# Channel-major projections: high and low part of the activations as one 512-column moving operand, small vectors loaded as rows, a ring of four weight buffers

## The chip, the cores and the metric

The kernel runs on one NeuronCore of a Trainium2 chip. The metric is the device time of one execution in microseconds (us), the median of several runs.

The engines that matter are the tensor engine (PE; its loads of stationary operands are listed as PEld), the vector engine (DVE), the scalar engine (ACT), GpSimd (POOL) and the queue of the sync engine (SP), which issues nearly all transfers. Each takes its instructions in the order in which they stand in the program.

## The reference, cut to what matters

Two blocks follow each other, each with two layers, on 256 rows of width 1024, all in fp32. The first block has three attention branches, the second a mixer with three branches and a gated feed-forward part.

```python
# first block, layer l: x is 256 x 1024
h = rms_norm(x, norm_g[l])
q_a, k_a, v_a, q_h, f_h, i_h, q_m, z = split(h @ w_in[l])        # 512 columns each, z 1536
o_h = hgrn2_chunkwise(q_h, f_h, i_h, lb_all[l])                  # wants q_h and f_h with channels on partitions
kv_m = rms_norm(mem, mem_norm_g[l]) @ w_mem_kv[l]
x = x + (concat([o_a, o_h, o_m]) * silu(z)) @ w_out[l]

# second block, layer l
h = rms_norm_2(x, mix_pre_norm[l])
dn_qkv, dn_z, dn_b, dn_a, ret_q, ret_k, ret_v, ret_g, pool_u, gates = split(h @ w_in[l])
qkv = silu(causal_depthwise_conv(dn_qkv, dn_conv[l]))            # four taps along the rows, per channel
o_dn = gated_delta_rule(q, k, v, beta, g); ...                   # and retention, pooling
x = x + rms_norm_2(mixed @ w_out[l], ...);  x = x + rms_norm_2(swiglu(...), ...)
```

## The kernel before

**Products.** Every fp32 product is made of three matmuls on rounded parts: high weight times high activation, low times high, high times low. The activations stand transposed in SBUF as `aTh` (high) and `aTl` (low), channels on the partitions. `tok` products have the rows of x on the output partitions and move 512 weight columns per matmul. `chan` products have output channels on the partitions: the weight is the stationary operand, 128 channels at a time, and the 256 rows of `aTh` or `aTl` move. `chan` is called ten times: for f_h and then q_h in each layer of the first block, and for k, q and v of the gated delta branch (`dn_k`, `dn_q`, `dn_v`) in each layer of the second.

**One chan call.** It takes four weight units of 256 input by 512 output channels, and its 512 output channels are four blocks of 128. Two blocks share one PSUM bank. The call goes over the four units twice, once for each pair of blocks; a unit comes free in the second pass. After a pass the work on the result (`evac`: `hgrn_f`, `silu`, `conv_silu`) is queued, and reads the bank in PSUM. `conv_silu` makes for each block one ACT instruction with the first tap and three DVE instructions with the others, then a clamp and a silu.

**Weights.** `Stream` brings 412 units of 512 KB in a fixed order. SP loads a unit into one of five raw buffers; ACT copies it, rounded, to `wh`; DVE subtracts to give `wl`; PE uses both. There are six slots for such pairs, with two spare ones for some units. The slot of a unit is free for another when the last matmul on it is done. A raw buffer is free when its `wl` is done.

**What sets the order.** The class `Order` plans as the program is written: each piece of work on ACT and DVE is a generator that yields the tiles it needs, and is stepped when the planned time of PE has come so far. `pump` writes the splits of the weights among them. A scheduler then moves instructions within each engine, matmuls of two PSUM banks among each other as well.

**Small vectors.** Gains, convolution taps and the like are loaded with one element per partition (`(k p) -> p k`), most of them by SP between the weight loads, the first gain by POOL. `lower_bounds` and `mem_norm` load theirs about 40 us into the execution, `mixer2` loads `dn_conv`, `dn_out_norm` and `pool_scale` for its layer.

Of the kernel before, what the change touches and what calls it, by code (L numbers as in the profile page):

```python
# [35 lines left out]
K4, K2, SM, ACC = 11, 22, 24, 3  # L36
# [194 lines left out]
class Stream:  # L231
# [5 lines left out]
    RAW, SLOTS, SPARE, AHEAD = 5, 6, 2, 6  # L237
# [130 lines left out]
class Kernel:  # L368
# [50 lines left out]
    def part(self):  # L419

        return tuple(self.t(self.p_aT, [P, 4, S], tag, F32R) for tag in ("aTh", "aTl"))
# [121 lines left out]
    def norm(self, x, gb, hT, t, ss=None, gc=None):  # L543
# [19 lines left out]
        for b in range(2):  # L563
# [4 lines left out]
            for k in range(4):  # L568
                g = gc[:, 4 * b + k : 4 * b + k + 1]
                h, l = (y[:, k, t * P : (t + 1) * P] for y in hT[b])  # L570
# [61 lines left out]
    def tok(self, hT, keys, evac, own=True, wait=None, first=False):  # L632
# [4 lines left out]
        for t in range(NT):  # L637
# [4 lines left out]
            for key in keys:  # L642
                ps = self.acc()
                for u in range(nu):
                    if t == 0:
                        w[key, u] = self.stream.take((key, u))
                    for k in range(2):
                        kk = 2 * u + k
                        self.mm3(ps, tuple(x[:, kk % 4, t * P : (t + 1) * P] for x in hT[kk // 4]),
                                 tuple(x[:, k, :] for x in w[key, u]), kk == 0, kk == 2 * nu - 1)  # L650
# [5 lines left out]
    def chan(self, hT, key, evac):  # L656

        self.join_hT(0, 1)
        nu, ku, nj = KD // 2, 2, 4
        w = []  # L660
        for p in range(nj // 2):
            pt = self.acc((P, 2, S))
            for u in range(nu):
                if p == 0:
                    w.append(self.stream.take((key, u)))
                wh, wl = w[u]
                for k in range(ku):
                    kk = u * ku + k
                    xh, xl = (x[:, kk % 4, :] for x in hT[kk // 4])
                    for j in range(2):  # L670
                        c = slice((2 * p + j) * P, (2 * p + j + 1) * P)
                        o = pt[:, j, :]
                        first = kk == 0 and j == 0
                        last = kk == nu * ku - 1 and j == 1
                        self.pe.matmul(o, wh[:, k, c], xh, start=first, stop=False, skip_group_check=True)
                        self.pe.matmul(o, wl[:, k, c], xh, start=False, stop=False, skip_group_check=True)
                        self.pe.matmul(o, wh[:, k, c], xl, start=False, stop=last, skip_group_check=True)
                    self.o.poll()
                if p == nj // 2 - 1:
                    self.stream.free()  # L680
            self.o.spawn(evac(p, pt))
            self.o.poll()

    def out_proj(self, parts, skew, evac):
# [7 lines left out]
        def mm(t, n, i):  # L692
# [6 lines left out]
            for kk in range(2):  # L699
                xs = tuple(o[:, 2 * k + kk, t * P : (t + 1) * P] for o in oT)  # L700
# [56 lines left out]

    def constants(self):

        a, dve = self.a, self.dve  # L760
        neg = self.k2([P, 2 * P], "stage")
# [57 lines left out]
    def lower_bounds(self):  # L819

        l0, l1, d, e = (self.cst([P, 4], n) for n in ("lb0", "lb1", "lbd", "lbe"))
        for l, t in enumerate((l0, l1)):
# [1068 lines left out]
```

## Time and profile before

| | |
|---|---|
| median of 3 runs | 1415.88 us (1415.46 to 1416.79) |
| the profiled execution | 1414.58 us |
| its span, first to last instruction | 1412.7 us |
| PE busy | 1383.5 us (98%), 7604 matmuls |
| DVE busy | 1017.0 us (72%) |
| ACT busy | 829.4 us (59%) |
| granted TensorE clock, mean | 0.999 |

Matmuls overlap: the mean duration of one in a list of groups is longer than the distance from its start to the start of the next. PE's pace is read from the starts in a timeline. A row of the timeline can stand for several equal instructions in a row (x2 and so on); its start is that of the first. PEclk 0.999 is the upper of the clock's two levels, 2.4 GHz, in nearly the whole span.

### The profile page before, as it was taken

The page shows a single profiled execution, that of the slowest core. Times are in us where ns is not written, and L with a number is a line of the kernel's source. Part 1 is how long each engine was busy: PE and PEld are TensorE (multiplying, and loading weights), DVE is VectorE, ACT ScalarE, POOL GpSimd, SP SyncE. Part 2 cuts the span into 40 slices and gives each one's busy share as a digit, 9 for nine tenths or more (in the row PEclk, how much of TensorE's full clock was granted, in tenths as well). Part 3 has the DMA queues.
Part 4 walks back from the last instruction along what each step waited for, and adds up shares of the span by engine and source line. Part 5 has one row for each costly group of instructions (what it writes and reads, how often), then busy time and mean ns, then how long its engine had stood idle before and what let it go on. Part 6 is the DMA issues. An engine that isn't in the chain of part 4 may idle for free.

```text
span 1412.7 us, 20443 instructions
## 1 busy us (share of the span) xinstructions
PE 1383.5 (98%) x7604; PEld 1164.6 (82%) x7604; DVE 1017.0 (72%) x1708; ACT 829.4 (59%) x1420; POOL 31.4 (2%) x66
## 2 busy tenths in 40 slices
PE   7999999999999999999999999999999999999998
PEld 5878888887888898888877888879888887788886
DVE  6698777679887698657777655687968567666564
ACT  6676565566765476556755544565665466555452
POOL 7100000000000000000000000000000000000000
PEclk9999999999999999999999999999999999999999
DMA  8863446555345354235665656645544357365551
GB/s 271 216 152 101 122 138 218 165 158 170 118 146 181 117 181 136 89 90 179 205 198 164 190 185 194 220 138 175 152 118 120 98 184 253 120 202 186 182 187 64
DMA packets 140916, 229.06 MB, mean 162 GB/s; under 512 B 28304, under 2 KB 34064, under 8 KB 140816
## 3 DMA queue, kind: packets, MB, share of 16 engines
q1 hardware_dynamic: 140752, 227.75, 52.2%
q8 instruction: 60, 0.98, 0.3%
q0 software_dynamic: 64, 0.01, 0.1%
q14 instruction: 40, 0.33, 0.1%
HBM read 226.67 MB, written 1.05 MB: 161 GB/s over the span
## 4 chain that ended last, share of the span: by engine, by line
PE 79%; DVE 6%; DMA 5%; ACT 4%; issue 3%; SPq 1%; DVEq 0%; ACTq 0%
PE acc L137 54%; PE mx L137 21%; PE mx L147 4%; DVE wl L109 3%; ACT wh L109 2%; DMA raw<-in_w_in 2%; DMA raw<-in_w_out 1%; DMA raw<-in_ffn_gate 1%; SPq L408 1%; ACT sg L109 1%; ACT junk L109 1%; DMA gqk<-in_moba_q_norm 0%; DVE x L109 0%; DVE hlf L109 0%; DMA stage<-in_c_negs 0%
## 5 line engine op out<-in xcount | busy, mean ns | idle before, releaser
L109 DVE TENSOR_TENSOR wl<-raw,wh 128x1024 fp32r<-128x1024 f32 x396 | 479.8, 1220 | 145.2 <-ACT wh L109 139.1
L109 ACT CAST wh<-raw 128x1024 fp32r<-128x1024 f32 x396 | 412.6, 1049 | 173.3 <-PE acc L137 91.9
L137 PE MATMUL acc<-wh,aTh 128*128 128x512 f32 x1232 | 494.6, 402 | 2.7 <-ACT aTh L109 2.6
L137 PE MATMUL acc<-wl,aTh 128*128 128x512 f32 x1232 | 485.2, 394 | 0.2 <-DVE wl L109 0.2
L137 PE MATMUL acc<-wh,aTl 128*128 128x512 f32 x1232 | 483.8, 393 | 1.0 <-DVE aTl L109 1.0
L137 PEld LDWEIGHTS acc<-wh,aTh 128*128 128x128 f32 x1232 | 232.1, 188 | 50.0 <-ACT aTh L109 4.8
L137 PEld LDWEIGHTS acc<-wh,aTl 128*128 128x128 f32 x1232 | 231.9, 188 | 49.7 <-DVE aTl L109 2.3
L137 PEld LDWEIGHTS acc<-wl,aTh 128*128 128x128 f32 x1232 | 232.3, 189 | 45.1 <-issue 1.0
L137 PE MATMUL mx<-wh,ff 128*128 128x512 f32 x352 | 111.2, 392 | 0.0
L137 PE MATMUL acc<-aTh,wh 128*128 128x256 f32 x320 | 91.0, 284 | 0.0
L137 PE MATMUL acc<-aTl,wh 128*128 128x256 f32 x320 | 90.6, 283 | 0.0
L137 PE MATMUL acc<-aTh,wl 128*128 128x256 f32 x320 | 90.5, 283 | 0.0
L137 PEld LDWEIGHTS mx<-wh,ff 128*128 128x128 f32 x352 | 65.6, 188 | 13.2
L109 ACT ACTIVATE sg<-sg 128x512 f32<-128x512 f32 (+1 forms) x120 | 73.7, 614 | 1.5
L109 ACT ACTIVATE sg<-zc 128x512 f32<-128x512 f32 (+1 forms) x60 | 37.0, 616 | 61.6 <-DVE zc L109 61.3
L137 PE MATMUL mx<-wl,ff 128*128 128x512 f32 x176 | 68.5, 389 | 0.0
L137 PEld LDWEIGHTS acc<-aTh,wh 128*128 128x128 f32 x320 | 61.3, 192 | 0.3
L137 PEld LDWEIGHTS acc<-aTh,wl 128*128 128x128 f32 x320 | 61.3, 192 | 0.2
L137 PEld LDWEIGHTS acc<-aTl,wh 128*128 128x128 f32 x320 | 61.3, 192 | 0.0
L109 DVE TENSOR_SCALAR zc<-acc 128x512 f32<-128x512 f32 (+1 forms) x48 | 31.9, 664 | 36.8 <-PE acc L137 36.8
L109 ACT CAST ff<-mx 128x256 fp32r<-128x256 f32 x44 | 14.4, 375 | 52.8 <-PE mx L147 52.8
L109 ACT CAST aTh<-mx 128x512 fp32r<-128x512 f32 x44 | 24.7, 585 | 31.9 <-PE mx L147 31.6
(313 smaller groups left out, 1656.0 us busy)
## 6 DMA issues: line engine op xcount, KB each, us to landing
raw<-in_w_in SPq DMA_DIRECT2D x200, 512.0 KB, 4.3
raw<-in_ffn_down SPq DMA_DIRECT2D x44, 512.0 KB, 4.8
raw<-in_w_out SPq DMA_DIRECT2D x40, 512.0 KB, 4.5
raw<-in_ffn_gate SPq DMA_DIRECT2D x40, 512.0 KB, 4.6
raw<-in_ffn_up SPq DMA_DIRECT2D x40, 512.0 KB, 4.5
raw<-in_w_mem_kv SPq DMA_DIRECT2D x16, 512.0 KB, 4.5
raw<-in_w_branch_pool SPq DMA_DIRECT2D x8, 512.0 KB, 3.7
raw<-in_w_branch_ret SPq DMA_DIRECT2D x8, 512.0 KB, 4.0
```

The costliest lines, as they stand in the source:

```text
L109: r = f(out, *args, **kw)
L137: self._ns.matmul(out, lhsT, rhs, **kw)
L147: self._ns.transpose(out, x, ident)
L408: self.nc.sync.dma_start(dst, src)
```

## The change

The high and low part of the activations become one tile, `aT`, with both parts next to each other for each group of 128 channels. In `chan` one matmul moves both parts, 512 columns, over the high weight, and a second moves the 256 columns of the high part over the low weight into the first half of the bank. A block now fills one bank by itself, so the call goes over its four units four times, and a unit comes free in the fourth pass. The two halves of a bank are added by the new `halves_sum`: ACT copies the first half to SBUF, DVE adds the second. The evac then reads SBUF; `hgrn_f` drops the copy that it made before.

`columns` loads vectors as rows of 128 into one tile, transposes them on PE and copies them out with DVE. It takes the place of nearly all loads with one element per partition; the first gain moves from the queue of POOL to that of SP. The ring of raw buffers goes from five to four, the pool of small tiles from 22 to 24.

```diff
-K4, K2, SM, ACC = 11, 22, 24, 3
+K4, K2, SM, ACC = 11, 24, 24, 3
...
-    RAW, SLOTS, SPARE, AHEAD = 5, 6, 2, 6
+    RAW, SLOTS, SPARE, AHEAD = 4, 6, 2, 6
...
-        return tuple(self.t(self.p_aT, [P, 4, S], tag, F32R) for tag in ("aTh", "aTl"))
+        x = self.t(self.p_aT, [P, 4, 2, S], "aT", F32R)
+        return x[:, :, 0, :], x[:, :, 1, :], x
...
-        for p in range(nj // 2):
+        for j in range(nj):
+            if j % 2 == 0:
+                self.uid += 1
+                banks, ready, out = [], f"chan{self.uid}", self.k2([P, 2, S], "chan")
             pt = self.acc((P, 2, S))
+            banks.append(pt)
+            c = slice(j * P, (j + 1) * P)
...
-                    xh, xl = (x[:, kk % 4, :] for x in hT[kk // 4])
-                    for j in range(2):
-                        c = slice((2 * p + j) * P, (2 * p + j + 1) * P)
-                        o = pt[:, j, :]
-                        first = kk == 0 and j == 0
-                        last = kk == nu * ku - 1 and j == 1
-                        self.pe.matmul(o, wh[:, k, c], xh, start=first, stop=False, skip_group_check=True)
-                        self.pe.matmul(o, wl[:, k, c], xh, start=False, stop=False, skip_group_check=True)
-                        self.pe.matmul(o, wh[:, k, c], xl, start=False, stop=last, skip_group_check=True)
+                    x = hT[kk // 4][2][:, kk % 4]
+                    self.pe.matmul(pt, wh[:, k, c], x, start=kk == 0, stop=False, skip_group_check=True)
+                    self.pe.matmul(pt[:, 0, :], wl[:, k, c], x[:, 0, :], start=False, stop=kk == nu * ku - 1, skip_group_check=True)
...
-                if p == nj // 2 - 1:
+                if j == nj - 1:
                     self.stream.free()
-            self.o.spawn(evac(p, pt))
+            if j % 2:
+                self.o.done.add(ready)
+            else:
+                self.o.spawn(self.chain(self.halves_sum(banks, ready, out), evac(j // 2, out)))
...
+    def halves_sum(self, banks, ready, out):
+        for j in range(2):
+            if j:
+                yield ready
+            yield banks[j]
+            self.act.copy(out[:, j, :], banks[j][:, 0, :])
+            yield out
+            self.dve.tensor_tensor(out[:, j, :], banks[j][:, 1, :], out[:, j, :], op=ALU.add)
+        yield out
...
+    def columns(self, dst, srcs):
+        r, n = self.k2([P, P], "rows"), 0
+        for src in srcs:
+            self.load(r[n : n + src.shape[0], :], src)
+            n += src.shape[0]
+        yield r
+        tp = self.mx((P, n))
+        self.pe.transpose(tp, r[:n, :], self.ident[:n, :n])
+        yield tp
+        self.dve.tensor_copy(dst[:, :n], tp)
+        yield dst
...
-        f, e, lf = self.k2(sh, "hf"), self.k2(sh, "he"), self.k2(sh, "hlf")
-        act.copy(f, ps)
-        yield f
+        f, e, lf = ps, self.k2(sh, "he"), self.k2(sh, "hlf")
...
-        for j in range(4):
-            self.load(cw[:, j, :], a["dn_conv_2"][l, j].rearrange("(i p) -> p i", p=P))
-        self.load(lay[:, 48:49], a["dn_out_norm_2"][l].unsqueeze(1))
-        self.load(lay[:, 60:64], a["pool_scale_2"][l].rearrange("(n p) -> p n", p=P))
+        o.spawn(self.columns(lay, [a["dn_conv_2"][l, j].rearrange("(i p) -> i p", p=P) for j in range(4)]
+                             + [a["dn_out_norm_2"][l : l + 1], a["pool_scale_2"][l].rearrange("(n p) -> n p", p=P)]), f"lay{l}")
...
-        self.nc.gpsimd.dma_start(gc, a["norm_g" if self.depth1 else "mix_pre_norm_2"][0].rearrange("(k p) -> p k", p=P))
-        o.ready[gc.name] = 4000.0
+        cols = self.columns(gc, [a["norm_g" if self.depth1 else "mix_pre_norm_2"][0].rearrange("(k p) -> k p", p=P)])
+        next(cols)
```

**On PE,** in the first layer of the second block, at the start of the call for `dn_v`. The numbers behind the names tell tiles apart; `acc` is a PSUM bank. Before, the call's first matmuls on its first unit (wh_5292 and wl_5293) read:

```order
L137 MATMUL acc_5459<-aTh_4723,wh_5292 128x256
L137 MATMUL acc_5459<-aTh_4723,wl_5293 128x256
L137 MATMUL acc_5459<-aTl_4724,wh_5292 128x256
L137 MATMUL acc_5459<-aTh_4723,wh_5292 128x256
L137 MATMUL acc_5459<-aTh_4723,wl_5293 128x256
L137 MATMUL acc_5459<-aTl_4724,wh_5292 128x256
```

After, the units of this call are 5168, 5179, 5270 and 5286, its blocks 5307, 5341, 5362 and 5390. Its first block at the third and fourth unit reads:

```order
L137 MATMUL acc_5307<-aT_4625,wh_5270 128x512
L137 MATMUL acc_5307<-aT_4625,wl_5271 128x256
L137 MATMUL acc_5307<-aT_4625,wh_5270 128x512
L137 MATMUL acc_5307<-aT_4625,wl_5271 128x256
L137 MATMUL acc_5341<-aT_4624,wh_5168 128x512
L137 MATMUL acc_5307<-aT_4625,wh_5286 128x512
L137 MATMUL acc_5341<-aT_4624,wl_5169 128x256
L137 MATMUL acc_5341<-aT_4624,wh_5168 128x512
...
L137 MATMUL acc_5307<-aT_4625,wl_5287 128x256
```

Three matmuls have become two, and seven matmuls of the second block (acc_5341) stand among those of the first block on the fourth unit, six of them between its high and its low weight.

**On ACT,** around the splits of the third and fourth unit of the same call, while PE ends the call for `dn_q`. Before (third and fourth unit: 5398, 5422; the two after them belong to the next product):

```order
L109 ACTIVATE conv_5370<-acc_5308,lay_4857 128x256 x2
L109 CAST wh_5398<-raw_5123 128x1024
L109 CAST wh_5422<-raw_5266 128x1024
L109 ACTIVATE sg_5408<-zc_5407 128x512
L109 CAST wh_5437<-raw_5290 128x1024
L109 ACTIVATE sg_5408<-sg_5408 128x512
L109 CAST wh_5452<-raw_5341 128x1024
L109 ACTIVATE sg_5408<-sg_5408 128x512
```

After (third and fourth unit: 5270, 5286):

```order
L109 COPY chan_5236<-acc_5237 128x256
L109 ACTIVATE sg_5274<-zc_5273 128x512
L109 CAST wh_5270<-raw_5164 128x1024
L109 ACTIVATE sg_5274<-sg_5274 128x512
L109 ACTIVATE conv_5281<-chan_5184,lay_4756 128x256
L109 ACTIVATE sg_5274<-sg_5274 128x512
L109 ACTIVATE conv_5281<-chan_5184,lay_4756 128x256
L109 CAST wh_5286<-raw_5189 128x1024
L109 CAST wh_5296<-raw_5198 128x1024
L109 CAST wh_5301<-raw_5218 128x1024
L109 COPY chan_5236<-acc_5262 128x256
```

The two casts stood next to each other; now four instructions of silu and convolution stand between them, and the copy of the fourth block of `dn_q` (acc_5262) stands behind three more casts.

**On DVE,** at the same place. Before:

```order
L109 TENSOR_TENSOR wl_5399<-raw_5123,wh_5398 128x1024
L109 SCALAR_TENSOR_TENSOR conv_5370<-acc_5308,lay_4857,conv_5370 128x254
L109 TENSOR_TENSOR wl_5423<-raw_5266,wh_5422 128x1024
L109 SCALAR_TENSOR_TENSOR conv_5370<-acc_5308,lay_4857,conv_5370 128x253
L109 TENSOR_TENSOR wl_5438<-raw_5290,wh_5437 128x1024
```

After:

```order
L109 TENSOR_TENSOR wl_5271<-raw_5164,wh_5270 128x1024
L109 SCALAR_TENSOR_TENSOR conv_5281<-chan_5184,lay_4756,conv_5281 128x255
L109 TENSOR_TENSOR cvk_5001<-zc_5273,sg_5274 128x512
L109 SCALAR_TENSOR_TENSOR conv_5281<-chan_5184,lay_4756,conv_5281 128x254
L109 SCALAR_TENSOR_TENSOR conv_5281<-chan_5184,lay_4756,conv_5281 128x255
L109 TENSOR_TENSOR wl_5287<-raw_5189,wh_5286 128x1024
L109 TENSOR_TENSOR wl_5297<-raw_5198,wh_5296 128x1024
L109 SCALAR_TENSOR_TENSOR conv_5281<-chan_5184,lay_4756,conv_5281 128x253
L109 SCALAR_TENSOR_TENSOR conv_5281<-chan_5184,lay_4756,conv_5281 128x254
L109 TENSOR_TENSOR wl_5302<-raw_5218,wh_5301 128x1024
L109 SCALAR_TENSOR_TENSOR conv_5281<-chan_5184,lay_4756,conv_5281 128x253
L109 TENSOR_TENSOR chan_5236<-acc_5262,chan_5236 128x256
```

One instruction of the convolution stood between the low parts of the third and fourth unit; now four instructions do. The sum that empties the bank acc_5262 stands behind three low parts and six others.

## Rows read from the trace of the kernel before

**Rows 1.** The page's first lines: span; busy time, share and count by engine.

```profile
span 1412.7 us, 20443 instructions
PE 1383.5 (98%) x7604; PEld 1164.6 (82%) x7604; DVE 1017.0 (72%) x1708; ACT 829.4 (59%) x1420; POOL 31.4 (2%) x66
```

**Rows 2.** Waits of PE: line, awaited engine: us in total, times, longest.

```profile
PE mx L147 <- DVE xn L109: 11.2, 6, 7.2
...
PE acc L137 <- DVE wl L109: 0.2, 1, 0.2
```

**Rows 3.** Timeline of PE, dn_q to dn_v: start, duration, instruction.

```profile
505.77 0.28 PE L137 MATMUL acc<-aTh,wl 128*128 128x256 f32 x1
...
506.49 0.28 PE L137 MATMUL acc<-aTh,wl 128*128 128x256 f32 x1
...
507.93 0.28 PE L137 MATMUL acc<-aTh,wl 128*128 128x256 f32 x1
```

**Rows 4.** Timeline of PE, a tok product of the first layer.

```profile
23.83 0.39 PE L137 MATMUL acc<-wh,aTh 128*128 128x512 f32 x1
...
26.10 0.62 PE L137 MATMUL acc<-wh,aTh 128*128 128x512 f32 x2
```

**Rows 5.** Groups by line and shape: count | busy us, mean ns | idle before.

```profile
L137 PE MATMUL acc<-wh,aTh 128*128 128x512 f32 x1232 | 494.6, 402 | 2.7 <-ACT aTh L109 2.6
...
L137 PE MATMUL acc<-aTh,wh 128*128 128x256 f32 x320 | 91.0, 284 | 0.0
...
L109 DVE TENSOR_TENSOR ff<-mx,ff 128x256 fp32r<-128x256 f32 x44 | 16.8, 420 | 21.1 <-ACT ff L109 21.1
...
L109 ACT CAST ff<-mx 128x256 fp32r<-128x256 f32 x44 | 14.4, 375 | 52.8 <-PE mx L147 52.8
...
L109 ACT COPY hf<-acc 128x512 f32<-128x512 f32 x4 | 2.3, 573 | 4.7 <-PE acc L137 4.7
```

**Rows 6.** Timeline of ACT, second pass of dn_q and first of dn_v.

```profile
499.37 1.05 ACT L109 CAST wh<-raw 128x1024 fp32r<-128x1024 f32 x1 [0.60 <-PE acc L137]
500.81 1.05 ACT L109 CAST wh<-raw 128x1024 fp32r<-128x1024 f32 x1 [0.39 <-PE acc L137]
501.76 0.63 ACT L109 ACTIVATE sg<-zc 128x512 f32<-128x512 f32 x1
...
505.73 0.63 ACT L109 ACTIVATE sg<-zc 128x512 f32<-128x512 f32 x1 [0.39 <-DVE zc L109]
506.26 0.46 ACT L109 ACTIVATE conv<-acc,lay 128x256 f32<-128x256 f32 x1
...
507.50 0.63 ACT L109 ACTIVATE sg<-sg 128x512 f32<-128x512 f32 x1
```

**Rows 7.** Timeline of DVE, the same stretch.

```profile
501.09 1.21 DVE L109 TENSOR_TENSOR wl<-raw,wh 128x1024 fp32r<-128x1024 f32 x1
502.23 0.47 DVE L109 SCALAR_TENSOR_TENSOR conv<-acc,lay,conv 128x254 f32<-128x254 f32 x1
502.62 1.21 DVE L109 TENSOR_TENSOR wl<-raw,wh 128x1024 fp32r<-128x1024 f32 x1
...
505.61 0.68 DVE L109 TENSOR_TENSOR cvk<-zc,sg 128x512 f32<-128x512 f32 x1
506.21 1.21 DVE L109 TENSOR_TENSOR wl<-raw,wh 128x1024 fp32r<-128x1024 f32 x1
```

**Rows 8.** Busy us of each engine by stretch, count; clock, DMA share, GB/s.

```profile
500.00:512.00 12.00, 12.00 (x102) 12.00 (x101) 11.55 (x22) 9.23 (x15) 0.00 (x0) 1.00 0.57 176
```

**Rows 9.** Timeline of all engines, the first 12.5 us.

```profile
1.25 1.09 POOL L1790 DMA_DIRECT2D gain<-in_norm_g  x1 [0.82 <-POOLq L1880]
1.63 0.42 SPq L408 DMA_DIRECT2D ident<-in_c_ident  x1
...
9.56 1.04 ACT L109 CAST wh<-raw 128x1024 fp32r<-128x1024 f32 x1 [3.49 <-DMA raw<-in_w_in]
...
11.94 0.79 PE L137 MATMUL acc<-wl,aTh 128*128 128x512 f32 x1 [0.22 <-DVE wl L109]
```

**Rows 10.** Timeline of PE, the transposes for the norm of mem.

```profile
54.89 0.88 PE L147 MATMUL mx<-ident,xn 128*128 128x128 f32 x6 [1.68 <-DVE xn L109]
```

More of the change, by code (lines that the diff above doesn't have):

```diff
@@ L569, in norm @@
                 g = gc[:, 4 * b + k : 4 * b + k + 1]
-                h, l = (y[:, k, t * P : (t + 1) * P] for y in hT[b])
+                h, l = (y[:, k, t * P : (t + 1) * P] for y in hT[b][:2])
                 self.act.activation(h, tp[b][:, k, :], AF.Copy, scale=g)
@@ L648, in tok @@
                         kk = 2 * u + k
-                        self.mm3(ps, tuple(x[:, kk % 4, t * P : (t + 1) * P] for x in hT[kk // 4]),
+                        self.mm3(ps, tuple(x[:, kk % 4, t * P : (t + 1) * P] for x in hT[kk // 4][:2]),
                                  tuple(x[:, k, :] for x in w[key, u]), kk == 0, kk == 2 * nu - 1)
@@ L699, in mm @@
             for kk in range(2):
-                xs = tuple(o[:, 2 * k + kk, t * P : (t + 1) * P] for o in oT)
+                xs = tuple(o[:, 2 * k + kk, t * P : (t + 1) * P] for o in oT[:2])
                 self.mm3(pss[t][i], xs, tuple(w[:, kk, :] for w in ws[n, i]),
@@ L756, in masks @@
         return t
+    def columns(self, dst, srcs):
[9 more added lines that the diff above has]
+        yield dst
     def constants(self):
         a, dve = self.a, self.dve
+        L = self.depth1
+        cut = lambda x: x.rearrange("(n p) -> n p", p=P)
+        c = self.cst([P, 32], "cols")
+        srcs = []
+        for l in range(L):
+            srcs += [a["mem_q_norm"][l : l + 1], a["mem_k_norm"][l : l + 1], a["hgrn_o_norm"][l : l + 1], cut(a["mem_norm_g"][l])]
+        srcs += [cut(a["hgrn_lb_logits"][l]) for l in range(2)]
+        yield from self.columns(c, srcs)
+        self.mem_qk, self.ogain = [c[:, 11 * l : 11 * l + 2] for l in range(L)], [c[:, 11 * l + 2 : 11 * l + 3] for l in range(L)]
+        self.mem_gain = [c[:, 11 * l + 3 : 11 * l + 11] for l in range(L)]
+        self.lb = [c[:, 11 * L + 4 * l : 11 * L + 4 * l + 4] for l in range(2)]
+        self.o.done.add("cols")
         neg = self.k2([P, 2 * P], "stage")
@@ L871, in mem_norm @@
     def mem_norm(self, mT):
-        self.mem_gain = [self.cst([P, KD], f"memgain{l}") for l in range(self.depth1)]
-        for l, x in enumerate(self.mem_gain):
-            self.load(x, self.a["mem_norm_g"][l].rearrange("(k p) -> p k", p=P))
         for m in range(NT):
@@ L925, in layer1 @@
         ss = [self.sm(16, "qkss") for _ in range(NT)]
+        if not l:
+            o.join("cols")
         for n, x in enumerate("qk"):
@@ L1389, in dn_scalars @@
         for k in range(KD):
-            xh, xl = (x[:, k % 4, :] for x in hT[k // 4])
+            xh, xl = (x[:, k % 4, :] for x in hT[k // 4][:2])
             pe.matmul(ps, wh[:, k, :], xh, start=k == 0, stop=False)
```

17 lines of the change are left out of this document (7 added, 10 removed).

## The prediction

> **What bounds the kernel now.** I read the page's first lines, then what PE waits for, then timelines. PE is busy for 1383.5 of 1412.7 us [rows 1]; DVE at 72% and ACT at 59% are not the bound over the whole span. PE's waits are few: 11.2 us for `xn`, most of it the 7.2 us before the first transposes, and in the whole execution 0.2 us for a `wl` [rows 2]. So time is won only by giving PE less to do, and lost wherever something that was ready in time comes late. The profiled execution took 1414.58 us, its span 1412.7, so 1.9 us lie around the span; the median of the three runs, 1415.88, is 1.3 us above it. I work out differences and put them to the median.
>
> **The products.** Read from mean durations, the gain would be large: three matmuls at 284 ns are 852 ns, and 402 plus 284 are 686 [rows 5]; times 320 that is 53 us. But durations overlap: the pace is the distance between starts. In the `dn_q` to `dn_v` stretch 18 matmuls of 256 columns go from 505.77 to 507.93 us [rows 3]: 2.16/18 = 0.120 us each. In a `tok` product 10 of 512 go from 23.83 to 26.10 [rows 4]: 0.227 us each. Three of 256 are 0.360, one of 512 with one of 256 is 0.347. The 768 columns are the same; what falls away is what each matmul costs beyond its columns, 0.013 us. Rows 5 count 320 triples, so PE saves 320 x 0.013 = **4.2 us**, 0.3%, all of it on the path, since PE does not wait in this stretch (12.00 of 12 us busy [rows 8]).
>
> The Trainium skill, TensorE: Matmul & The Clock Gate, Back-to-back issue gap, gives an isolated warm gap of N/2.4 + 2.5 ns, so 215.8 ns for 512 and 109.2 for 256, and an estimate from that page is a saving of 2.5 ns a triple, 0.8 us in all. The rows show 227 and 120 ns, the trace does not agree, and I keep 4.2 us.
>
> **The slots of the weights.** The price is in the passes. Before, PE spent 12 matmuls, 1.44 us, on a unit in each of two passes; a unit's slot came free in the second pass, and the third unit of the next call, which takes the slot of the first of this one, was wanted five such steps later, 7.2 us. The rows show it: its cast starts at 499.37 just after PE lets go [rows 6], its low part takes 1.21 from 501.09 [rows 7] and ends at 502.30, and PE uses it at 506.49 [rows 3], 4.2 us later. The low part of the fourth unit ends at 503.83 [rows 7] for 507.93 [rows 3], 4.1 us. After, a unit takes 2 x 0.347 = 0.694 us of each of four passes, it is free in the fourth only, and five steps are 3.5 us. Of 4.2 and 4.1 us about 0.5 is left, for the same work on ACT and DVE. This holds at six transitions: f_h to q_h in two layers, k to q and q to v in two.
>
> And the work is not the same. Each call gets four copies of 128x256 from PSUM and four sums of that size, at 375 and 420 ns by the nearest rows, the `ff` copies and subtractions [rows 5]. For ten calls that is 15.0 us of ACT and 16.8 of DVE; only four `hf` copies of 573 ns go, 2.3 us [rows 5]. In the delta calls DVE is busy for 11.55 of 12 us already [rows 8], so 1.7 us more in each call must push something behind.
>
> I walked the changed order at `dn_q` to `dn_v`, first layer, with steps from start to start: cast 0.95 (500.81 to 501.76), silu, tap, silu, tap together 1.77 (505.73 to 507.50) [rows 6]; low part 1.14, convolution step 0.39, `cvk` 0.60 [rows 7]. Zero is the end of the third block of `dn_q`. Its slots come free at 0.69 and 1.39; PE wants the third unit of `dn_v` at 4.16, the fourth at 4.86. ACT first copies, then a silu waits for a clamp that DVE reaches at about 1.0, behind six convolution steps. The first cast runs from 1.6 to 2.6, its low part to 3.8: in time. The four small instructions between the casts bring the second to 4.4 to 5.4, its low part to 6.7. PE has one matmul of the next block to put in between, then waits 0.3 us for the cast; six more reach to about 6.7. Without them it would wait 1.8. Then the bank: the third block of `dn_v` needs the bank of acc_5262, whose sum stands behind two low parts and three convolution steps, 6.7 + 2 x 1.14 + 3 x 0.39 + 0.42 = 10.6, while PE comes there at about 9.2, after two more blocks and some small products of the retention. That is 1.4 us, so 1.7 at this transition.
>
> The same walk gives about 1.1 us at q to v in the second layer (the low parts of two units stand behind twelve convolution steps), 0.7 at q_h in the first layer, and 0.4 more before the transposes for the norm of mem, where DVE, in order, now also waits for the transpose of the vectors ahead of the `xn` that PE waits for [rows 10]. At k to q, and at q_h in the second layer, I find next to nothing. Sum: **+3.9 us**. The bounds are 0, if DVE runs half a microsecond less behind at each place, and 10.1 us, if all of the added 1.7 us of DVE in six calls lands on PE. I take the walk, nearer to the lower end, since it goes by the rows of the same stretch.
>
> **Vectors, ring and start.** The loads as rows add four transposes, some 0.1 us each as one of 256 columns is 0.12 [rows 3]: +0.4. The first gain now stands on SP behind `ident` and ahead of the first two weight transfers, one issue of 0.42 us [rows 9]. PE's first matmul on a low part, at 11.94, follows from the landing of the first weight, which ended ACT's wait at 9.56 [rows 9]; so up to +0.4. Against it, the gather of the first gain with 4-byte elements on POOL's queue (issued from 1.25 [rows 9]) no longer shares the engines; between -0.4 and +0.4 I take -0.1. Later small loads lie under waits of SP that cost nothing. Four buffers for five would make 35 of 412 casts start later when I replay SP's issues with landing times of the trace, but nearly all of these have microseconds of lead left: 0, with +1 as the upper end. Two more small tiles free nothing that PE waits for. Sum: **+0.3 us**.
>
> **The forecast** is -4.2 + 3.9 + 0.3 = 0.0 us: **1415.9 us**, no change. About 0.2%, 2.8 us, is what a measurement of this kernel can tell from none.
>
> **The rivals.**
>
> (a) The waits do not appear. For it: before, `wl` cost PE 0.2 us in all [rows 2], each wait I found is of about the size of the error in DVE's lag, and six hoisted matmuls already cover one. The evac also leaves PSUM earlier, since it reads SBUF. Against it: the slot's time is halved by arithmetic. It gives -4.2 + 0.3, with at most 1 us of waits: 1412 to 1413. Chance 0.32.
>
> (b) DVE becomes PE's bound in the calls, and the kernel is slower. The mechanism is one: a sum of 0.42 us stands in order between the low parts, and once a low part comes after its use, every later instruction of DVE in the call is on PE's path, as there is 0.45 us of idle in 12 [rows 8] against 1.7 us added. It decides when the 0.5 us of lead left per unit is gone at all six transitions. All of it: -4.2 + 10.1 + 0.3 = +6.2, 1422.1; two thirds of it +2.8. So 1418.7 to 1422. Chance 0.20.
>
> (c) The vectors or the four buffers hurt: a transpose of rows holds DVE or PE at the start of a mixer or in the first 60 us until the rows have landed, 3 us or more, since a late landing is also late for the splits queued behind on DVE. 1419. Chance 0.05.
>
> (d) The saving itself is other. If the 0.013 us belonged to something that stays, such as the change of the moving width between 512 and 256, PE would save nothing, and the waits would be left: 1420. Chance 0.03. If the mean durations did count, 53 us: 1363; the row sums of overlapping matmuls speak against it. Or a 512-column matmul next to a 256-column one could run faster than in rows 4: at the pace of 256 columns for both, 0.240 for 0.360, 38 us. Chance 0.01 for these two together. The last is beside a rule of the Trainium skill, TensorE: Matmul & The Clock Gate, Back-to-back issue gap, by which a stream with weight loads takes about 131 ns for N=512. The 227 ns here, in such a stream, do not agree.
>
> (e) The change does what it says: 640 matmuls stand where 960 did, in the order as built, so I give nothing to its not happening.
>
> **How the numbers follow.** The forecast case, 1413 to 1418.7, has 0.39. Faster by over 0.2% is (a) with nearly all its part below 1413.1, and the small part of (d): 0.33. Slower is (b), (c) and the rest of (d): 0.28. The range of 8 in 10 reaches from 1411.5, a little below (a), to 1421, inside (b).
>
> **What the profile of after would show.** Right on the products: rows of 512 and 256 columns, x320 each, starts 0.347 us apart per pair. Right on the slots: PE waits for `wl`, `wh` or the sum on `chan`, 2 to 6 us in all, at `dn_q` to `dn_v` (near 504 and 981 us) and q_h; leads of some 0.5 us where there were 4. (a) shows no such rows, and the span shorter by 4. (b) shows the waits at all six, above 7 us, with DVE at 98% there. (c) shows waits for `rows` or a copy behind them. The prediction is wrong if the starts are not 0.347 apart, or if PE's waits for the split weights and banks in these calls come to under 1 us or over 7.

## The result, and the profile after

The changed kernel takes 1424.95 us, the median of six runs (1422.71 to 1429.67), against 1416.34 (1415.25 to 1418.76) for the kernel before, timed beside it. The ratio is 1.0071, 95% interval 1.0057 to 1.0085: **slower by 0.7%**, 8.6 us. The forecast was no change, 1415.9 us, with 1421 as the upper end of the range.

The profiled execution took 1425.68 us, 11.1 more than that of before. The first lines of the page of after, against [rows 1]:

```profile
span 1423.9 us, 19892 instructions
PE 1387.3 (97%) x7288; PEld 1151.4 (81%) x7288; DVE 1026.7 (72%) x1747; ACT 839.1 (59%) x1461; POOL 28.1 (2%) x65
```

Though PE has 316 matmuls less, it is busy for 3.8 us more (1387.3 for 1383.5), and it is idle for 36.6 us (1423.9 - 1387.3) where it was idle for 29.2. So the change lost time in two ways: 7.4 us in which PE waits, and something that makes PE's own work longer. The mean granted clock tells what the second is: 0.995, before 0.999.

The groups of after that answer to [rows 5]: count, then busy us and mean ns of one, then the idle time of the engine ahead of them.

```profile
L137 PE MATMUL acc<-aT,wh 128*128 128x512 f32 x320 | 115.0, 402 | 0.6 <-DVE chan L109 0.6
L137 PE MATMUL acc<-aT,wl 128*128 128x256 f32 x320 | 90.3, 284 | 0.2 <-DVE wl L109 0.2
...
L109 DVE TENSOR_TENSOR chan<-acc,chan 128x256 f32<-128x256 f32 x40 | 16.4, 417 | 8.9 <-ACT chan L109 8.5
...
L109 ACT COPY chan<-acc 128x256 f32<-128x256 f32 x40 | 14.5, 367 | 26.2 <-PE acc L137 26.0
```

The products are as the diff says, and the new copies and sums cost what the nearest rows gave (375 and 420 ns forecast, 367 and 417 measured). PE waited 0.6 us for a sum and 0.2 for a low part in the whole execution. Of the 3.9 us of waits that I had priced, 3.5 were for these, in the calls; they are not there. What PE waits for instead, from the list of its waits in after (us in total, times, longest), beside [rows 2]:

```profile
PE mx L147 <- DVE xn L109: 6.9, 6, 2.5
PE mx L147 <- DMA rows<-in_norm_g: 5.9, 1, 5.9
...
PE mx L147 <- ACT pexp L109: 2.0, 1, 2.0
...
PE mx L137 <- DVE pT L109: 1.5, 1, 1.5
PE mx L137 <- DMA pw<-in_pool_w: 1.3, 1, 1.3
...
PE mx L137 <- ACT pT L109: 0.7, 1, 0.7
...
PE acc L137 <- DVE chan L109: 0.6, 1, 0.6
PE acc L137 <- DVE wl L109: 0.2, 1, 0.2
```

The 5.9 us for `rows` only take the place of the 7.2 for `xn` at the start. New are the waits for `pexp` and `pT`, tiles of the memory attention, which the prediction does not name at all. They stand close together, in the second layer of the first block. PE's timeline of after there (start, duration, instruction, count, and in brackets the idle time ahead and what ended it):

```profile
410.20 0.40 PE L137 MATMUL acc<-wh,aT 128*128 128x512 f32 x1
412.08 1.16 PE L137 MATMUL mx<-vm,pT 128*128 128x128 f32 x8 [1.48 <-DVE pT L109]
413.07 1.03 PE L137 MATMUL mx<-kmT,qmT 128*128 128x256 f32 x4
416.08 1.24 PE L147 MATMUL mx<-ident,pexp 128*128 128x128 f32 x4 [1.98 <-ACT pexp L109]
418.06 2.08 PE L137 MATMUL mx<-vm,pT 128*128 128x128 f32 x8 [0.74 <-ACT pT L109]
419.93 1.91 PE L147 MATMUL mx<-ident,y 128*128 128x128 f32 x8
421.63 1.79 PE L137 MATMUL mx<-kmT,qmT 128*128 128x256 f32 x4
422.99 0.67 PE L137 MATMUL acc<-wh,aT 128*128 128x512 f32 x1
```

From 410.2 to 423.0 us there is not one product. Six steps of the attention stand in a row, and ahead of three of them PE waits for what ACT or DVE has to make first (1.48, 1.98 and 0.74 us). In the kernel before the same kinds of step stand between products, which fill the time (its timeline of PE):

```profile
413.07 1.05 PE L137 MATMUL mx<-vm,pT 128*128 128x128 f32 x8
413.96 1.03 PE L137 MATMUL mx<-kmT,qmT 128*128 128x256 f32 x4
414.64 0.58 PE L137 MATMUL mx<-wh,aTh 128*128 128x512 f32 x1
...
418.74 0.60 PE L147 MATMUL mx<-ident,pexp 128*128 128x128 f32 x4
419.09 0.48 PE L137 MATMUL mx<-wh,aTh 128*128 128x512 f32 x1
```

And the clock. In after the eight `vm,pT` at 412.08 take 1.16 us and the same eight at 418.06 take 2.08; the four `kmT,qmT` 1.03 and then 1.79. Busy us of each engine by stretches of 5 us (PE, PEld, DVE, ACT, POOL, with counts), then the granted clock, DMA share, GB/s; of after:

```profile
50.00:55.00 5.00, 2.32 (x12) 1.59 (x12) 4.96 (x9) 2.31 (x5) 1.29 (x1) 0.95 0.81 236
55.00:60.00 5.00, 5.00 (x24) 4.43 (x23) 4.63 (x9) 3.71 (x8) 0.00 (x0) 0.71 0.82 207
...
410.00:415.00 5.00, 2.62 (x15) 1.74 (x13) 4.80 (x8) 3.08 (x8) 0.00 (x0) 1.00 0.80 258
415.00:420.00 5.00, 3.12 (x13) 2.43 (x14) 4.68 (x15) 3.47 (x8) 0.00 (x0) 0.63 0.36 117
420.00:425.00 5.00, 5.00 (x21) 4.39 (x20) 2.98 (x6) 1.46 (x3) 0.00 (x0) 0.68 0.00 0
```

and of before:

```profile
50.00:55.00 5.00, 3.32 (x28) 3.12 (x28) 3.79 (x12) 2.76 (x6) 0.71 (x2) 1.00 0.69 213
55.00:60.00 5.00, 5.00 (x43) 5.00 (x44) 4.96 (x9) 3.25 (x6) 0.00 (x0) 1.00 0.61 161
```

After PE had waited 1.5 and 2.0 us with twelve small matmuls between, the clock fell to its lower level, 1.2 GHz, for a large part of the ten microseconds from 415; likewise after the wait of 2.5 us for `xn` at 54.34, where before had one of 1.68 [rows 10] and no fall. (0.63 is a mean of the two levels, 1 and 0.5.) What full speed would have given and these four stretches did not is 5 x (0.05 + 0.29 + 0.37 + 0.32) = 5.2 us, an upper bound of the loss, since PE was idle in part of it. This is most of the added PE time: at most 5.2 us, less the 2.2 that the products save (below), is 3.0 of the 3.8 us.

**Where along the execution.** I compared, between two profiles, the start of the first matmul on the same weight unit; the lag is how much later it is in after. At units 48, 80, 128, 208 and 411 of 412 (194, 291, 476, 764 and 1396 us) it is 1.6, 2.4, 10.4, 11.5 and 11.3 us. So 8 us are lost between 291 and 476, in the second layer of the first block, and the whole second block, where six of the ten changed calls are, loses 1.

### The profile page after: what moved, and what is told of

It is laid out like the page before. It is cut to its first block, busy times and chain, and to the rows that moved or that the text cites. A ratio compares the mean times of both kernels' runs of the same rounds, so it can differ in the third digit from the quotient of the medians.

```text
span 1423.9 us, 19892 instructions
## 1 busy us (share of the span) xinstructions
PE 1387.3 (97%) x7288; PEld 1151.4 (81%) x7288; DVE 1026.7 (72%) x1747; ACT 839.1 (59%) x1461; POOL 28.1 (2%) x65
## 4 chain that ended last, share of the span: by engine, by line
PE 85%; DVE 5%; DMA 4%; ACT 4%; issue 2%; SPq 0%; DVEq 0%; ACTq 0%
PE acc L137 59%; PE mx L137 21%; PE mx L147 5%; DVE wl L109 2%; ACT wh L109 2%; DMA raw<-in_w_out 1%; DMA raw<-in_ffn_up 1%; DMA raw<-in_w_in 1%; ACT junk L109 1%; DMA pw<-in_pool_w 0%; ACT sg L109 0%; DMA rows<-in_norm_g 0%; ACT aT L109 0%; DVE on L109 0%; DVE chan L109 0%
## 5 line engine op out<-in xcount | busy, mean ns | idle before, releaser
L137 PE MATMUL acc<-wh,aT 128*128 128x512 f32 x2464 | 797.4, 397 | 2.0 <-ACT aT L109 1.9
L137 PEld LDWEIGHTS acc<-wh,aT 128*128 128x128 f32 x2464 | 461.5, 188 | 96.2 <-ACT aT L109 3.7
L137 PE MATMUL acc<-wl,aT 128*128 128x512 f32 x1232 | 485.0, 394 | 0.0
L137 PEld LDWEIGHTS acc<-wl,aT 128*128 128x128 f32 x1232 | 232.3, 189 | 45.3 <-issue 0.7
L137 PE MATMUL acc<-aT,wh 128*128 128x512 f32 x320 | 115.0, 402 | 0.6 <-DVE chan L109 0.6
L137 PE MATMUL acc<-aT,wl 128*128 128x256 f32 x320 | 90.3, 284 | 0.2 <-DVE wl L109 0.2
L137 PEld LDWEIGHTS acc<-aT,wh 128*128 128x128 f32 x320 | 60.5, 190 | 15.0 <-ACT chan L109 0.9
L137 PEld LDWEIGHTS acc<-aT,wl 128*128 128x128 f32 x320 | 60.9, 190 | 1.2 <-DVE wl L109 0.8
L137 PE MATMUL mx<-wh,aT 128*128 128x512 f32 x160 | 52.1, 394 | 0.0
L109 DVE TENSOR_SCALAR zc<-acc 128x512 f32<-128x512 f32 (+1 forms) x44 | 29.2, 663 | 28.4 <-PE acc L137 28.2
L137 PEld LDWEIGHTS mx<-wl,ff 128*128 128x128 f32 x176 | 33.1, 188 | 6.8
```

The source lines that it names most:

```text
L109: r = f(out, *args, **kw)
L137: self._ns.matmul(out, lhsT, rhs, **kw)
```

## The experiments

All were timed in five rounds against the kernel before. The theories ahead of the first runs: V, the vectors as rows and the start cost the time; R, the four raw buffers or the 24 tiles; S, the passes and slots cost in the calls, which is the price of the prediction; O, the loss lies in the order that the planner writes for the attention branches of the first block. Formed after the first four runs, H: the new sums on DVE push back the chain of small work in the first block. Formed after the next four, P, which is O made definite: the extra work changes the order that the planner writes, and it is this order, not the work, that leaves PE without products. All results, with the lag behind before in the profiles:

| run | median us | ratio, 95% interval | lag at unit 80 | 128 | 411 |
|---|---|---|---|---|---|
| after | 1424.95 | 1.0071 (1.0057 to 1.0085) | 2.4 | 10.4 | 11.3 |
| vec_only | 1416.35 | 1.0007 (0.9998 to 1.0016) | -2.4 | -2.0 | -0.1 |
| chan_only | 1418.77 | 1.0032 (1.0021 to 1.0044) | -0.2 | 5.5 | 4.7 |
| ring_only | 1414.56 | 0.9992 (0.9978 to 1.0007) | -2.0 | -2.9 | -1.2 |
| ring5 | 1423.0 | 1.0055 (1.0040 to 1.0070) | 1.4 | 6.6 | 8.6 |
| new_second_block | 1414.81 | 1.0003 (0.9992 to 1.0014) | -1.2 | -1.6 | 0.8 |
| new_first_block | 1422.48 | 1.0053 (1.0036 to 1.0070) | 1.8 | 7.0 | 8.5 |
| copies_only_first | 1415.46 | 1.0002 (0.9991 to 1.0012) | 1.0 | 0.6 | -0.3 |
| no_sums_first | 1420.65 | 1.0046 (1.0030 to 1.0061) | -3.6 | 4.7 | 5.7 |
| first_block_slack400 | 1412.71 | 0.9986 (0.9978 to 0.9995) | 0.6 | -2.2 | -1.7 |
| after_slack400 | 1418.99 | 1.0024 (1.0014 to 1.0035) | 0.7 | 0.4 | 2.0 |
| after_slack50 | 1422.73 | 1.0051 (1.0036 to 1.0067) | 2.2 | 4.3 | 4.7 |
| before_slack50 | 1425.47 | 1.0072 (1.0059 to 1.0086) | -0.6 | 10.4 | 12.3 |
| before_margin400 | 1413.04 | 0.9973 (0.9960 to 0.9987) | 0.9 | -2.4 | -1.3 |
| chan_margin400 | 1410.73 | 0.9959 (0.9944 to 0.9974) | 1.1 | -2.1 | -2.9 |
| chan_ring_margin400 | 1419.41 | 1.0019 (1.0004 to 1.0033) | 1.2 | 1.7 | 2.1 |

The lags are those of one profiled execution each. For after_slack400, after_slack50 and chan_ring_margin400 it is the shortest or the second shortest of all, 2.6, 3.7 and 2.9 us below the median, so the lag of a usual execution is probably larger there.

**One part of the change alone.** The vectors, the products, and the ring with the tiles were each put by themselves on the kernel before, and the ring was taken out of the change.

```diff
 # vec_only
+        yield from self.columns(c, srcs)
-            self.load(t, self.a["hgrn_lb_logits"][l].rearrange("(n p) -> p n", p=P))
 # chan_only: the hunks of chan, halves_sum, hgrn_f and aT
+                    self.pe.matmul(pt, wh[:, k, c], x, start=kk == 0, stop=False, skip_group_check=True)
 # ring_only (on before); ring5 is after with these two lines as in before
-K4, K2, SM, ACC = 11, 22, 24, 3
+K4, K2, SM, ACC = 11, 24, 24, 3
-    RAW, SLOTS, SPARE, AHEAD = 5, 6, 2, 6
+    RAW, SLOTS, SPARE, AHEAD = 4, 6, 2, 6
```

> The kernel before with only the vectors loaded as rows (products, five raw buffers and 22 small tiles as before). Theory V (the rows' transposes hold DVE and PE at 50 to 60 us, and the lower clock after the stall at 54 us costs more): some 3 us slower than before, about 1419, with the 2.7 us stall before the xn transposes near 54 us and a granted clock below 1.00 behind it. Theory O (the loss comes from the order that the planner writes for the attention branches of the first block, which the new products upset): within 2 us of before, 1414.5 to 1418. Theory R (ring of four): no change.

> The kernel before with only the new products and their sums (vectors, five raw buffers, 22 small tiles as before). Theory O: 4 to 8 us slower than before, 1420 to 1424, with the stalls in the first block outside the chan calls (around the attention branches, 320 to 425 us) and under 2 us of PE waits for wl, wh or chan. Theory S (slots, the price that I forecast): slower or equal with over 3 us of PE waits for wl, wh or chan at the calls. Theory V: 3 to 4 us faster than before, 1412 to 1413.

> The kernel before with only four raw buffers and 24 small tiles. Theory R: slower by 3 us or more, 1419 and up. Theories O, V and S: within 2 us of before, 1414 to 1418, since nearly all casts that would start later have leads of microseconds.

> The changed kernel with five raw buffers and 22 small tiles again. Theory R: back to about 1416 or below. Theories O, V and S: stays at 1421 to 1427; by O it may move by some us either way, since the order that is written changes with the ring too.

Vectors and ring change nothing that can be measured when alone, so V falls, and R as a cost of its own on this kernel. The products alone cost 0.32%, and the place is the one of after: a lag of -0.2 at unit 80 and 5.5 at unit 128. chan_only has the same stretch without products and the same fall of the clock (0.69 from 410 to 415, 0.62 from 415 to 420). Two signs went the other way: the time, 1418.77 us, is below the 1420 to 1424 of O, and PE waits 4.1 us for low parts and sums, where over 3 us was the sign of S. Nearly all of it, 1.57 and 1.77 us at 50.94 and 58.31, stands at f_h to q_h in the first layer, and at unit 80 the kernel is still not behind before. Together the parts cost more than their sum, 0.0071 against 0.0007 + 0.0032 - 0.0008, so a price for each part doesn't explain the whole.

**The two blocks apart.** `chan_old` is the `chan` of before; one kernel uses it for f_h and q_h, the other for `dn_k`, `dn_q` and `dn_v`. Both have five raw buffers and 22 tiles.

```diff
 # new_second_block
-        self.chan(hT, (l, "f_h"), lambda j, ps: self.hgrn_f(l, j, ps, A[j], kx[j]))
+        self.chan_old(hT, (l, "f_h"), lambda j, ps: self.hgrn_f(l, j, ps, A[j], kx[j]))
 # new_first_block
-            self.chan(hT, (l, "dn_" + n),
+            self.chan_old(hT, (l, "dn_" + n),
```

> The new products and sums in the second block only (k, q, v); f_h and q_h by the old products, vectors and buffers as before. Theory H (in the second layer of the first block the added copies and sums hold up the hgrn2 chain on a DVE that is over 90% busy there; PE runs out of other work 100 us later, near 405 to 425 us, and its clock drops): no such stall, no clock drop, 1412 to 1415, 1 to 2.5 us faster than before. Theory S (the passes and slots cost in every call): 1417 or more, since six of the ten calls are here.

> The new products and sums for f_h and q_h only. Theory H: carries the whole loss, 1419 to 1422, with the waits of PE near 405 to 420 us and the granted clock below 0.8 behind them. Theory S: a smaller part of the loss, 1416 to 1418, since only four of the ten calls are here.

S falls for the second block: with six of the ten calls changed, among them the four transitions k to q and q to v, the time is that of before. The four calls of the first block give 0.53% of the 0.71%. No saving shows there either: a new wait of 1.3 us for `pw`, whose load SP issues at 547.47 us where it was 542.37 in before, stands against the 1.3 us that 192 pairs gain at the pace measured below.

**Is it the work of the sums?** copies_only_first keeps the old products in the first block and adds the copies and DVE passes (a maximum of a value with itself). no_sums_first has the new products there without the DVE additions: the matmuls are all made, but the second half of each bank, high weight times low activation, is left out of the result.

```diff
 # copies_only_first
+            self.act.copy(out[:, j, :], pt[:, j, :])
+            self.dve.tensor_tensor(out[:, j, :], pt[:, j, :], out[:, j, :], op=ALU.max)
 # no_sums_first
-            self.dve.tensor_tensor(out[:, j, :], banks[j][:, 1, :], out[:, j, :], op=ALU.add)
```

> The kernel before with its old products; in the calls of the first block each finished bank is copied to SBUF by two ACT copies and two DVE passes of 128x256 (the maximum of the bank and the copy, which changes nothing), as many and as large as the copies and sums of the change, and the rest reads the copy. Theory H: these alone bring the loss, 1418 to 1423, and PE's wait near 405 to 420 us. If it is the new products with their four passes that bring it: 1414 to 1417, no such wait.

> As the one with the new products in the first block only, without the DVE sums there: the ACT copies stay, the product of high weight and low activation is left out of f_h and q_h. Theory H: the hgrn2 chain starts earlier and the loss shrinks, 1412 to 1417. If the passes bring it: 1419 to 1422 as with the sums.

H falls from both sides. All of the added work without the new products costs nothing (1.0002), although it makes the chain of the block late: the `hST` matmuls start at 402.57 there, at 390.36 in before. The new products without the DVE work cost 0.46%. In no_sums_first the attention again stands bare, earlier, with waits of 2.8 us for `pexp` and 2.3 for `pT`, and the clock is at its lower level throughout (0.50 and 0.52):

```profile
405.00:410.00 5.00, 1.24 (x4) 0.57 (x4) 4.41 (x11) 3.51 (x9) 0.00 (x0) 0.50 0.40 117
410.00:415.00 5.00, 4.49 (x18) 4.03 (x19) 1.90 (x2) 0.46 (x1) 0.00 (x0) 0.52 0.36 105
```

**Is it the order?** The planner steps a piece of work when its planned input time is at most `SLACK`, 200 ns, past PE's planned time; what is left when a stage has no more products is written in a row. A larger margin writes the steps earlier, among the products. The splits of the weights go by the same margin, so the whole order of the layer moves with it, not that of the attention alone. The edit takes nothing from the work and is made in one layer only, the second of the first block: the first line stands at the start of each layer of that block (with 50.0 for 400.0 in the two runs named 50), the second ahead of the second block.

```diff
+        self.o.SLACK = 400.0 if l else 200.0
+        self.o.SLACK = 200.0
```

> New products and sums in the first block only, as before, but the planner's margin (the lead by which work of ACT and DVE is written ahead of PE's planned time) is 400 instead of 200 in the second layer of that block alone: the same instructions, another order, in which products stand between the steps of the memory attention again. Theory P (the loss is the written order: a row of dependent steps of the memory attention with no product between them): no wait of 2 to 3 us near 403 to 418 us, no clock drop, 1414 to 1418 against 1422.5 with 200. Theory S (four passes, slots): stays at 1420 to 1424.

> The changed kernel whole, with the same margin of 400 in the second layer of the first block. Theory P: 1416 to 1420, 5 to 8 us below the changed kernel, with only the clock drop near 55 us left. Theory S: 1422 to 1427.

> The changed kernel whole with a margin of 50 in that layer; here too no row of three or more steps of the memory attention stands without a product. Theory P: below the changed kernel by some us, 1416 to 1422, more uncertain since work of ACT and DVE is written later. Theory S: 1422 to 1427.

> The kernel before, with a margin of 50 in the second layer of the first block: old products, old sums, but an order in which four steps of the memory attention stand in a row with no product between. Theory P: 3 to 8 us slower than before, 1418 to 1423, with waits for pexp and pT near 400 to 425 us and a lower clock behind them. Theory S: within 2 us of before.

> The kernel before with the margin of 400 in the second layer of the first block and nothing else. If the gain of first_block_slack400 (ratio 0.9986) is the products': 1414 to 1417, no change. If it is the margin's: 1411.5 to 1413.5.

first_block_slack400 is new_first_block with this line. Its ratio goes from 1.0053 to 0.9986, 9.8 us by the medians, at the same products, sums and copies; 1412.71 us is below even the 1414 to 1418 of P, since the margin brings 2.7 us (1415.76 - 1413.04) to the kernel before as well. The windows of first_block_slack400 show PE covered and the clock up:

```profile
410.00:415.00 5.00, 5.00 (x29) 4.27 (x28) 5.00 (x9) 4.43 (x9) 0.00 (x0) 1.00 0.62 192
415.00:420.00 5.00, 4.65 (x27) 3.78 (x26) 4.24 (x7) 4.37 (x9) 0.00 (x0) 1.00 0.55 143
```

The converse was made on the kernel before, with its old products: a margin of 50 instead of 200 in that layer makes it as slow as the change, 1.0072, more than the 1418 to 1423 us that P gave, with the loss in the same layer. Its windows:

```profile
400.00:405.00 5.00, 5.00 (x28) 5.00 (x28) 2.12 (x5) 0.40 (x1) 0.00 (x0) 0.57 1.01 364
...
410.00:415.00 5.00, 2.06 (x8) 1.01 (x8) 4.71 (x15) 2.54 (x8) 0.00 (x0) 0.61 0.37 92
415.00:420.00 5.00, 4.82 (x18) 4.36 (x19) 1.99 (x4) 0.27 (x2) 0.00 (x0) 0.50 0.30 120
```

And its timeline of PE at the bare steps:

```profile
398.33 1.97 PE L137 MATMUL mx<-v_sb,pT 128*128 128x64 f32 x8 [2.94 <-DVE pT L109]
...
410.79 0.83 PE L147 MATMUL mx<-ident,y 128*128 128x128 f32 x4 [1.79 <-DVE y L109]
413.27 1.23 PE L147 MATMUL mx<-ident,pexp 128*128 128x128 f32 x4 [1.65 <-ACT pexp L109]
415.18 2.08 PE L137 MATMUL mx<-vm,pT 128*128 128x128 f32 x8 [0.68 <-ACT pT L109]
417.05 1.91 PE L137 MATMUL mx<-kmT,qmT 128*128 128x256 f32 x4
418.76 1.91 PE L147 MATMUL mx<-ident,y 128*128 128x128 f32 x8
420.60 0.80 PE L137 MATMUL acc<-wh,aTh 128*128 128x512 f32 x1
```

The last of these are the steps of after, without any of the change; here the stretch without products is longer, from 394.56 to 420.60, and takes in steps of the other attention (`v_sb,pT`) and of hgrn2. So P is shown in both directions.

after_slack50 missed its range: 1422.73 us is above the 1416 to 1422 of P and inside that of S. Its trace speaks for P all the same. The expectation had ruled out a bare row of the memory attention; from 401.39 to 412.05 there is one of both attentions together, with waits of 1.08, 0.78 and 1.06 us and a lower clock behind them:

```profile
401.39 0.40 PE L137 MATMUL acc<-wh,aT 128*128 128x512 f32 x1
402.87 0.66 PE L147 MATMUL mx<-ident,pexp 128*128 128x128 f32 x4 [1.08 <-ACT pexp L109]
...
406.48 1.09 PE L147 MATMUL mx<-ident,pexp 128*128 128x128 f32 x4 [1.06 <-ACT pexp L109]
...
412.05 0.50 PE L137 MATMUL acc<-wh,aT 128*128 128x512 f32 x1 [0.34 <-ACT aT L109]
```

```profile
405.00:410.00 5.00, 3.83 (x17) 3.08 (x17) 4.41 (x14) 2.56 (x9) 0.00 (x0) 0.72 0.66 234
```

In the seventeen traces such a row goes with a loss of 0.3% and more. Past the first 60 us, seven have a stretch of over 7 us without a product: after 12.8 us, chan_only 13.0, new_first_block 12.7, ring5 12.2, no_sums_first 17.0, before_slack50 26.0 and after_slack50 10.7, each in the second layer of the first block and with waits of PE in it. These are the seven kernels with a ratio of 1.0032 and more. In the other ten the longest is 6.9 us, and PE does not wait in it.

The margin alone is worth 0.27% to the kernel before. It takes back two thirds of what the change lost (after_slack400, 1.0024). But at the same margin before stands at 0.9973, so the whole change still costs 0.5% there, with no bare row left. One fall of the clock remains, to 0.77 and 0.89 from 50 to 60 us, after a wait of 2.87 us for `xn` at 53.21; it is worth 1.7 us at most.

**What the products are worth in a covered order.** Two kernels with the margin of 400: the new products alone on before, and these with the ring and tiles of the change.

```diff
 # chan_ring_margin400 against chan_margin400
-K4, K2, SM, ACC = 11, 22, 24, 3
+K4, K2, SM, ACC = 11, 24, 24, 3
-    RAW, SLOTS, SPARE, AHEAD = 5, 6, 2, 6
+    RAW, SLOTS, SPARE, AHEAD = 4, 6, 2, 6
```

> New products and sums in all ten calls with the margin of 400; vectors, five raw buffers and 22 small tiles as before. If rows and ring carry the rest of the changed kernel's loss: 1410 to 1413, below both kernels (first_block_slack400 at 1412.7, less up to 1 us for the second block). If the products carry it: 1417 to 1420 as after_slack400.

> As chan_margin400, with four raw buffers and 24 small tiles. If the ring costs nothing: within 1.5 us of chan_margin400, and the rows are what is left between this and after_slack400, by the stall before the xn transposes near 53 us and the lower clock behind it. If the ring costs: 1415 to 1419.

chan_margin400 is faster than both kernels: 1410.73 us, 0.9959. Against before_margin400 the medians differ by 1413.04 - 1410.73 = 2.3 us. The intervals of the two ratios overlap, and the two orders have other waits and other falls of the clock as well, so this is no measurement of the products alone.

The ring and the tiles, which cost nothing on the kernel before, cost 8.7 us by the medians here, a little more than the 1415 to 1419 us given for a ring that costs. chan_ring_margin400, without the vectors, has the ratio of after_slack400 with them (1.0019 and 1.0024), so what is left of the change at this margin goes with the ring and the tiles. The profiles show 5.0 us of the 8.7. The two kernels are level at unit 80, and 3.8 us come before unit 128, where PE waits 0.9 us for `hZ` and 1.3 for `pexp` that chan_margin400 does not wait for. The profiled execution of chan_ring_margin400 has a mean clock of 0.998 and the median one of 0.996, so part of the rest may be clock; no trace shows it. Whether the buffers themselves or the order written for them do this, no run tells, and it stays open.

## Why the prediction was wrong, by its steps

**The products: right in kind, half the size.** Triples started 0.360 us apart [rows 3]. Pairs in the same calls of after:

```profile
513.49 0.40 PE L137 MATMUL acc<-aT,wh 128*128 128x512 f32 x1
513.72 0.28 PE L137 MATMUL acc<-aT,wl 128*128 128x256 f32 x1
513.84 0.40 PE L137 MATMUL acc<-aT,wh 128*128 128x512 f32 x1
...
514.55 0.40 PE L137 MATMUL acc<-aT,wh 128*128 128x512 f32 x1
```

From 513.49 to 514.55 are three pairs, 0.353 each; over all undisturbed pairs of the trace the mean is 0.352, not 0.347. In the mean the low-weight matmul follows 0.235 us after the wide one, where 0.227 was forecast, and the wide one 0.117 after it. So the saving is about 320 x 0.007 = 2.2 us instead of 4.2. The 2.3 us between before_margin400 and chan_margin400 are as large, but that is partly luck, as said. The mis-sized term is 320 x 0.013: I took paces from streams of one width and added them for a stream that alternates. By the Trainium skill, TensorE: Matmul & The Clock Gate, Back-to-back issue gap, an estimate for the pair is 215.8 + 109.2 = 325 ns; the trace, with 353, does not agree.

**The slots: lead as worked out, waits not.** The lead of the low part over its first use, in the third and fourth unit of `dn_v`, went from 4.2 and 4.1 us to 1.2 and 0.2 in the first layer, and to 0.8 and 0.6 in the second: the 0.5 that I expected. But at `dn_q` to `dn_v` PE did not wait; the 1.7 us there, and the bank wait in it, did not come, and for the whole execution 0.8 us stand against the 3.5 of the calls. Under 1 us was the prediction's own sign of being wrong. The walk put four small ACT instructions between the two casts and the sum behind two low parts; as built, the sums came in time. So rival (a), the waits do not appear, had the right mechanism at this place; with a saving of 2.2 its sum gives about 1414, not 1412 to 1413. In chan_margin400, which is the faster kernel, PE waits 2.2 us for low parts and 2.5 for sums, most of it at f_h to q_h in the first layer, a transition at which I had found 0.7, and behind them the clock falls to 0.94 and 0.71 from 55 to 65 us. Against this stand shorter waits for `xn` and none for `hZ`.

**Rivals (b) and (c) name the right sign and the wrong mechanism.** The time came out above the range of (b), but DVE did not become PE's bound in the calls: at dn_q to dn_v, eleven us later than before, it is busy for 10.47 of 12 us where [rows 8] had 11.55. The windows of after:

```profile
512.00:524.00 12.00, 12.00 (x69) 10.47 (x68) 10.47 (x19) 9.04 (x17) 0.00 (x0) 1.00 0.58 175
```

And the transitions of the second block cost nothing in new_second_block. On the kernel before, (c) falls with vec_only and ring_only; with the new products in a covered order the ring and the tiles did cost (chan_ring_margin400), and the waits that its trace has more are for `hZ` and `pexp`, not for landings.

**The step that failed** is one that the sum does not have. I priced each edit against the order as it stood in before and looked for the change of order only in and around the calls. The order outside is made anew from planned times, and four passes with their copies are enough, even without the sums (no_sums_first), to move steps of the attention out from between the products. The rows for it were within reach, since the order of the changed kernel could be read: PE's sequence of after has `vm,pT`, `kmT,qmT`, `ident,pexp`, `vm,pT`, `ident,y`, `kmT,qmT` with no product between, and that of before has no such row. Its price, which the sum put at nothing, follows from the timelines: about 4.2 us of waits (1.48 + 1.98 + 0.74), where before had 1.2 at 404.89, and up to 3.5 us of lower clock, 6.5 of the 8 us that were lost there. The second missing term is the clock: I had given the longer wait for `xn` 0.4 us; it was 0.8 longer (2.5 for 1.68) and up to 1.7 us of lower clock followed. DVE's three low parts, two of which had waited for other things, stand ahead of `xn` in the trace, in order, so the wait was of the kind named and the price was not.

Why four passes at equal work lead the planner to this order, and why the margin of 400 does not, was not traced through its planned times; the runs show that the loss goes with the order. The 0.5% that the change costs at the margin of 400 on both sides goes with the ring and the tiles, and how is open.

## What to carry to other kernels

Where a planner or scheduler orders the instructions, a change of a few microseconds moves work far from the edit, and here a planner's margin alone moved the time by 12 us (1413.0 to 1425.5) with the same work. So read the order as built over the whole program for places where the busiest engine has a row of dependent steps with no independent work between, whichever branches the steps belong to, before pricing the edit itself, and compare variants only after each has had its order set right. Price such a row at its waits and the clock that falls behind it; and take a pace from a stream of the same mix of widths.

## What the runs showed of the hardware

The clock's price was new to me. Each fall was found behind a wait of PE of some 1 to 3 us, and as the microseconds at 1.2 GHz that follow are ones in which PE is busy, the loss comes behind the wait, in work that itself waits for nothing: `mx<-vm,pT` x8 in 2.08 us for 1.16. In after, chan_only, new_first_block, ring5, no_sums_first, before_slack50 and after_slack50 such waits stand close together with only small matmuls between.

A wait alone does not tell whether the clock falls. In before, with waits of up to 1.7 us past the start, it is 1.00 in every 5 us; in after one of 1.8 us for `hZ` at 321.45 brings no fall, nor does one of 3.0 us at 77.06 in chan_ring_margin400. But a single wait among products brought one in copies_only_first (1.94 us at 81.71, clock 0.74 and 0.92 from 80 to 90) and in before_slack50 (2.86 us at 1198.89, 0.96 and 0.70 from 1195 to 1205). What decides between them no run here shows.

The other is the pace of matmuls of alternating width: 0.353 us for 512 and 256 columns, where streams of one width gave 0.227 and 0.120.
